# A Trainium2 encoder layer: the accumulating DMAs that make the weights' low parts read SBUF instead of DRAM, and make more of those parts

## The chip, the cores and the metric

The kernel runs on one core of one Trainium2 chip. The metric is the device time of one execution in microseconds (us), lower being better. The core has a matrix engine (PE, whose weight loads the profile lists apart as PEld), a vector engine (DVE), a scalar engine (ACT), a general engine (POOL) and a queue engine (SP) that here only issues DMAs. Every engine works through its own list of instructions in order, and semaphores tie the lists together. DMAs issued by SP, ACT and POOL share 16 DMA engines.

## What is computed

One layer of a bidirectional encoder is run on two requests with the same weights: the first request P has 512 tokens, the second, S, has 1024, with 1024 features each, all in float32.

```python
def encoder_layer(h, p_l, ...):
    u = group_rmsnorm(h, norm_mix_pre)
    proj = u @ w_in                              # 1024 x 5664: z, xBC, dt, hyena columns
    ...
    # SSD heads: depthwise conv + SiLU, chunked scans forward and backward,
    #   gate with silu(z), grouped norm
    # Hyena heads: depthwise conv, long convolution by FFT, grouped norm
    mix = jnp.concatenate([y_ssd, y_hy], axis=-1) @ w_out          # 2048 x 1024
    h = h + group_rmsnorm(mix, norm_mix_post)
    u = group_rmsnorm(h, norm_ffn_pre)
    ff = (jax.nn.silu(u @ w_gate) * (u @ w_up)) @ w_down           # hidden 2816
    h = h + group_rmsnorm(ff, norm_ffn_post)
    gate = jax.nn.sigmoid((group_rmsnorm(h, ple_norm_pre) @ w_ple_gate))
    e = p_l @ w_ple_proj
    return h + group_rmsnorm(gate * e, ple_norm_post)
```

## The kernel before

**Three products for one.** Every large matrix product is made of three. Each operand is split into a high part, its value rounded to the matrix format `F32R`, and a low part, what the rounding left. `mm3` (L296) then adds high times high, high times low and low times high in PSUM. On the activations' side `split_ps` (L324) makes the parts: the high one on ACT (L325), the low one on DVE (L326). On the weights' side there are two ways:

- `split_w` (L289): ACT copies the staging tile `wst` into `whi` (L292), and POOL subtracts, `wlo = wst - whi` (L293, a TENSOR_TENSOR).
- `split_dma` (L280): ACT writes `-wst`, rounded, into `wlo` (L284), then POOL issues a DMA with an adding destination that adds the exact weight on top (L285), and ACT copies `wst` into `whi` (L286). What is added comes from DRAM: the same rows of the weight that `wst` was loaded from.

`load_w` (L260) loads one block of a weight in two halves, each through `raw_w` (L275), a DMA of SP into a `wst` tile of 256 KB (128 partitions x 512 values). It chooses between the two ways: `split_w` where columns of another weight are put beside (`extra`, in `project_z` alone, 264 instead of 256 columns) or once `pool_lo` is set, else `split_dma`. `wst`, `whi` and `wlo` have six buffers each and are shared by the whole kernel, so a load must wait for whoever reads the tile six loads earlier.

**The stages.** First the projections of P, then of S, with `w_in` (192 tiles); beside them, as a second stream with PSUM of its own, the filters, the SSD scans and the long convolutions. From L1423 on the tail: P's output projection (`outproj`), P's FFN (`ffn`) beside the long convolution of S, then `pool_lo = True` (L1441), and the tail of S: the output projection in two groups of 512 tokens (`out_group`), P's embedding gate (`ple`) in between, gate and up products (`gate_up`, Strassen-like sums of weight blocks, which call `raw_w` and `split_w` themselves), the down projection (`down_group`), the embedding gates of S.

**The streamed products.** `out_group` and `down_group` go through `stream_gemm` (L1152). There the activations are loaded too: one row, a DMA of SP of 256 KB into one of two `mx` buffers (L1187), is split by ACT into `mh` and by DVE into `ml` (three buffers each), and takes part in 12 products with one weight tile. There are 152 rows: 64 in the output projection (2 groups x 2 halves of the columns x 16) and 88 in the down projection (2 x 2 x 22). SP issues the loads of `mx` and `wst` by turns.

The order of the instructions on each engine is made by the framework's scheduler when the program is built, from its own costs; tiles wait for each other by semaphores.

Of the kernel before, what the change touches and what calls it, by code (L numbers as in the profile page):

```python
# [15 lines left out]
ALU = mybir.AluOpType  # L16
# [66 lines left out]
class Whole:  # L83


    def __init__(self, his, los):
        self.parts, self.w = (his, los), his[0].shape[1]
# [79 lines left out]
class Kern:  # L167
    def __init__(self, ctx, tc, ins, outs, cst):
        self.ctx, self.tc, self.nc, self.I, self.cst = ctx, tc, tc.nc, ins, cst
        self.P = Seq("p", LP, ins["x_prompt"][0], ins["p_prompt"][0, 0], outs[0][0])  # L170
        self.S = Seq("s", LS, ins["x_sample"][0], ins["p_sample"][0, 0], outs[1][0])
        self.n = 0
        self.wide_tail = self.pool_lo = False
        for q in (self.P, self.S):
            d = lambda nm, shp: tc.dram_tile(shp, F32, name=f"{nm}_{q.nm}")
            L, R = q.L, q.R
            q.xs = d("xs", [L, 1024])
            q.z = d("z", [L, 1024])
            q.bt = d("bt", [2, 128, L])
            q.ct = d("ct", [2, 128, L])  # L180
            q.bk = d("bk", [L, 256])
            q.rows = d("rows", [2, q.nc, 16, 128])
            q.g = d("g", [R, 128, 1024])
            q.x0 = d("x0", [R, 128, 1024])
            q.K = d("K", [8, 128, R * 2 * 128])
            q.mix = d("mix", [16, 128, L])
            q.h1 = d("h1", [L, 1024])
            q.h2 = d("h2", [L, 1024])
            q.e = d("e", [L, 1024])
        self.S.hid = tc.dram_tile([NF, 128, LS], F32, name="hid_s")  # L190
# [69 lines left out]
    def load_w(self, src, a, b, extra=None):  # L260

        nc = self.nc
        rows = []
        n = max(1, a // 2)
        for k in range(0, a, n):
            ks = slice(k, k + n)
            w = src.shape[-1]
            st = self.raw_w(src[:, ks], b)
            if extra is not None:
                nc.gpsimd.tensor_copy(st[:, :, w:], extra[:, ks])  # L270
            hi, lo = self.split_w(st) if extra is not None or self.pool_lo else self.split_dma(st, src[:, ks])
            rows += [(hi[:, i], lo[:, i]) for i in range(n)]
        return rows

# [2 lines left out]
        self.nc.sync.dma_start(st[:, :, :src.shape[2]], src)  # L277
        return st

    def split_dma(self, w, src):  # L280

        nc = self.nc
        hi, lo = (self.T(self.wp, list(w.shape), t, F32R, 6) for t in ("whi", "wlo"))
        nc.scalar.activation(lo, w, AF.Copy, scale=-1.0)  # L284
        nc.gpsimd.dma_start(lo[:, :, :src.shape[2]], src, accum_op=ALU.add)  # L285
        nc.scalar.activation(hi, w, AF.Copy)  # L286
        return hi, lo

# [1090 lines left out]
    def build(self):  # L1379
# [40 lines left out]
        def tags(pool, *sizes):  # L1420
            return {t: (pool, t, n) for t, n in sizes}

        with self.pool("mix_s", side="right") as mp, ExitStack() as right:  # L1423
            pm = tags(mp, ("mx", 2), ("mh", 3), ("ml", 3))
            tr = right.enter_context(self.pool("out_s", side="right"))
            po = pm | tags(tr, ("acc", 4), ("row", 2), ("t4", 2), ("junk", 1), ("stage", 2), ("wsum", 1))
            with self.pool("tail_u") as tu, self.pool("tail_p") as tp:
                pl = tags(tu, ("et", 2), ("hh", 4), ("hl", 4), ("t4", 2), ("uh", 2), ("ul", 2))
                pl |= tags(tp, ("acc", 4), ("mst", 1), ("row", 2), ("junk", 1))
                pl["mx"] = pl["t4"]  # L1430
                pl["ga"] = pl["acc"]
                pt = self.ple_in(pl, [(S, 1)], True)
                mix = self.mix_in(P, 0, pl, 0, 8)
                self.ple_proj(pl, [(S, 1)], pt)
                acc = self.new_acc(pl)
                self.outproj(P, 0, pl, acc, 0, mix)
                pt = self.ple_in(pl, [(P, 0), (S, 0)])
                u = self.outproj(P, 0, pl, acc, 8, self.mix_in(P, 0, pl, 8, 8), lambda: self.new_u(pl, 4))
                self.ple_proj(pl, [(P, 0), (S, 0)], pt)
                u = self.ffn(P, 0, pl, u)  # L1440
                self.pool_lo = True  # L1441
                acc = self.new_acc(po)
                out = self.out_group(S, 0, po, acc)
                next(out)
                self.ple_post(P, 0, pl, self.ple(P, 0, pl, u))
            self.apool = self.pools["x"][0]
            next(out)
            with self.pool("blocks") as tb:
                pb = pm | tags(tb, ("bh", 14), ("bl", 14))
                po |= pb  # L1450
                us = [self.out_post(S, 0, po, acc)]
                acc = self.new_acc(po)
                for _ in self.out_group(S, 1, po, acc):
                    pass
                us.append(self.out_post(S, 1, po, acc))
                right.close()
                with self.pool("hid_s", side="right") as tr:
                    ph = pb | tags(tr, ("wsum", 3), ("sc", 5), ("gt", 6))
                    pe = pb | {"wsum": pm["mx"], "gt": pm["mh"], "sc": pm["ml"]}
                    both = dict(enumerate(us))  # L1460
                    self.gate_up(S, [(p, m, {g: both[g] for g in gs}) for p, gs, ms in (
                        (pe, [0], (0, 2)), (ph, [1], (0, 2)), (ph, [0, 1], range(4, NF, 2))) for m in ms])
                with self.pool("end_s", side="right") as tr:
                    pe = pb | tags(tr, ("row", 3), ("t4", 3), ("junk", 1), ("mst", 2))
                    pe |= {"acc": pe["bl"], "ga": pe["bh"]}
                    self.wide_tail = True
                    vs = [self.down_group(S, g, pe, lambda: Quarters(
                        *[[self.T(pe, [128, 4, 256], t, F32R) for _ in range(4)] for t in ("bh", "bl")]))
                        for g in range(2)]
                    for g in range(2):  # L1470
                        self.ple_post(S, g, pe, self.ple(S, g, pe, vs[g]))
# [30 lines left out]
```

## Time and profile before

| | |
|---|---|
| median of 3 runs | 2881.7 us (2876.18 to 2881.93) |
| the profiled execution | 2865.54 us, its span 2863.7 us, mean granted PE clock 0.977 |
| instructions in the span | 41893 |
| HBM read, written | 430.43 MB, 91.95 MB |

The profiled execution is 16.2 us (0.56%) faster than the median of the runs. Sums made from the profile are made against its 2865.54 us.

How to read it: the page gives the busy time of each engine, then the span in 40 slices of 71.6 us with the busy share in tenths. Roughly, slices 0 to 23 hold the projections and P's tail, 24 to 28 the output projection of S, 29 to 34 its gate and up products, 35 to 38 its down projection and embedding gates. Groups of instructions are named by line, engine, operation and by what they write and read. "mean ns" is the time of one. A wait row such as `PE g L301 <- ACT mh L325: 17.1, 8, 7.4` reads: PE sat idle before instructions of L301 until ACT's L325 had ended, 17.1 us in all, 8 times, 7.4 us at the longest. A name with a q behind it (SPq) is the engine's queue, which issues.

### The profile page before, as it was taken

Reading aid. Unit: us, or ns where it says so; the run is one execution under the profiler, and the core shown is the slowest. Engines: PE = TensorE matmul, PEld = TensorE weight load, DVE = VectorE, ACT = ScalarE, POOL = GpSimd, SP = SyncE. Lnnn points to the kernel's source line nnn. Section 1 sums busy time; section 2 is a strip of 40 time slices with the busy share of each in tenths; the row PEclk is TensorE's granted clock in tenths of the full one; section 3 lists DMA queues with packets and bytes.
Section 4 is the critical chain, followed back from the end, with each engine's and each line's share of the span. In section 5 each row is a group of like instructions: output and inputs, shape, how many; then the busy total and the mean of one; then the engine's idle time right before and its main releaser. Section 6 shows DMA issues by size and latency. Waiting matters only on the chain.

```text
span 2863.7 us, 41893 instructions
## 1 busy us (share of the span) xinstructions
PE 2682.8 (94%) x14696; PEld 2265.0 (79%) x14696; DVE 1696.4 (59%) x2905; ACT 1418.8 (50%) x2747; POOL 1388.6 (48%) x1147
## 2 busy tenths in 40 slices
PE   6999999999999988989999998989789999999998
PEld 5887898778888766777788776767689999877776
DVE  4675786886565684765576665365853434224345
ACT  5555545774335575674444454455543333345443
POOL 3444544343443443544465555554674445435464
PEclk8999999999999998989999999999899999999999
DMA  9799956978768898989999997475332222366665
GB/s 221 193 206 199 217 180 168 259 176 178 145 141 180 197 289 245 232 242 223 188 199 224 189 208 239 137 237 159 120 98 82 80 79 82 107 210 202 213 202 187
DMA packets 565261, 525.16 MB, mean 183 GB/s; under 512 B 31985, under 2 KB 455737, under 8 KB 562747
## 3 DMA queue, kind: packets, MB, share of 16 engines
q1 hardware_dynamic: 344523, 348.39, 40.2%
q0 software_dynamic: 141504, 112.22, 24.8%
q10 hardware_dynamic: 79024, 61.88, 6.7%
q8 instruction: 116, 1.90, 0.3%
q14 instruction: 94, 0.77, 0.1%
HBM read 430.43 MB, written 91.95 MB: 182 GB/s over the span
## 4 chain that ended last, share of the span: by engine, by line
PE 39%; DVE 7%; DMA 4%; issue 4%; POOL 2%; ACT 1%; SPq 0%; ACTq 0%; POOLq 0%; DVEq 0%
PE g L301 10%; PE g L303 10%; PE g L302 9%; PE a L301 2%; PE a L302 2%; PE a L303 2%; DMA mx<-mix_s 1%; PE a L700 1%; DVE ml L326 1%; PE a L973 1%; DVE b L692 1%; DMA b<-g_s 1%; POOL wlo L293 1%; DVE t L1055 1%; POOL rs_t L309 1%
## 5 line engine op out<-in xcount | busy, mean ns | idle before, releaser
L293 POOL TENSOR_TENSOR wlo<-wst,whi 128x512 fp32r<-128x512 f32 (+1 forms) x378 | 538.8, 1431 | 512.0 <-ACT whi L292 482.2
L301 PE MATMUL g<-uh,whi 128*128 128x512 f32 (+1 forms) x1232 | 494.5, 401 | 10.0 <-DVE cv L393 8.3
L302 PE MATMUL g<-ul,whi 128*128 128x512 f32 (+1 forms) x1232 | 491.9, 399 | 0.3 <-DVE ul L326 0.3
L303 PE MATMUL g<-uh,wlo 128*128 128x512 f32 (+1 forms) x1232 | 490.7, 399 | 0.0
L292 ACT ACTIVATE whi<-wst 128x512 fp32r<-128x512 f32 (+1 forms) x378 | 236.4, 629 | 356.6 <-PE g L302 193.2
L286 ACT ACTIVATE whi<-wst 128x512 fp32r<-128x512 f32 x316 | 197.5, 626 | 252.4 <-PE g L302 187.5
L301 PE MATMUL g<-bh,whi 128*128 128x256 f32 x1056 | 295.7, 285 | 22.7 <-DVE rs_t L308 6.8
L285 POOL DMA_DIRECT2D wlo<-in_w_in x144 | 188.7, 1377 | 245.8 <-ACT wlo L284 211.7
L303 PE MATMUL g<-bh,wlo 128*128 128x256 f32 x1056 | 295.4, 282 | 2.9 <-POOL wlo L293 2.9
L302 PE MATMUL g<-bl,whi 128*128 128x256 f32 x1056 | 296.5, 282 | 0.0
L301 PEld LDWEIGHTS g<-uh,whi 128*128 128x128 f32 x1232 | 233.9, 190 | 68.9 <-ACT cv L387 7.8
L302 PEld LDWEIGHTS g<-ul,whi 128*128 128x128 f32 x1232 | 233.4, 189 | 55.5 <-issue 7.0
L303 PEld LDWEIGHTS g<-uh,wlo 128*128 128x128 f32 x1232 | 232.9, 189 | 53.4 <-issue 5.1
L326 DVE TENSOR_TENSOR ml<-mx,mh 128x512 fp32r<-128x512 f32 x152 | 125.5, 827 | 222.2 <-ACT mh L325 222.2
L393 DVE SCALAR_TENSOR_TENSOR cv<-g,cols,cv 128x510 f32<-128x510 f32 (+3 forms) x192 | 193.9, 1010 | 100.6 <-ACT cv L387 98.3
L284 ACT ACTIVATE wlo<-wst 128x512 fp32r<-128x512 f32 x316 | 195.7, 620 | 94.2 <-PE g L302 86.0
L301 PEld LDWEIGHTS g<-bh,whi 128*128 128x128 f32 x1056 | 198.4, 190 | 29.2 <-DVE rs_t L308 7.1
L303 PEld LDWEIGHTS g<-bh,wlo 128*128 128x128 f32 x1056 | 200.6, 190 | 3.2 <-POOL wlo L293 3.2
L302 PEld LDWEIGHTS g<-bl,whi 128*128 128x128 f32 x1056 | 200.9, 190 | 0.1
L309 POOL TENSOR_TENSOR rs_t<-rs_t,nhalf 128x1 f32<-128x1 f32 (+2 forms) x112 | 127.2, 1137 | 149.1 <-DVE rs_t L308 148.5
L301 PE MATMUL g<-whi,uh 128*128 128x264 f32 (+1 forms) x576 | 192.8, 337 | 3.4 <-ACT acc L1097 3.4
L302 PE MATMUL g<-wlo,uh 128*128 128x264 f32 (+1 forms) x576 | 191.5, 333 | 3.1 <-DMA wlo<-in_w_out 3.1
(331 smaller groups left out, 6375.2 us busy)
## 6 DMA issues: line engine op xcount, KB each, us to landing
wst<-in_w_in SPq DMA_DIRECT2D x192, 256.0 KB
wlo<-in_w_in POOLq DMA_DIRECT2D x144, 256.0 KB, 6.0
wst<-in_w_down SPq DMA_DIRECT2D x132, 256.0 KB
wst<-in_w_out SPq DMA_DIRECT2D x96, 256.0 KB
wst<-in_w_gate SPq DMA_DIRECT2D x96, 256.0 KB
wst<-in_w_up SPq DMA_DIRECT2D x96, 256.0 KB
mx<-hid_s SPq DMA_DIRECT2D x88, 256.0 KB
rw<-rows_s SPq DMA_DIRECT2D x32, 512.0 KB
```

Source lines behind the costliest of these rows:

```text
L284: nc.scalar.activation(lo, w, AF.Copy, scale=-1.0)
L285: nc.gpsimd.dma_start(lo[:, :, :src.shape[2]], src, accum_op=ALU.add)
L286: nc.scalar.activation(hi, w, AF.Copy)
L292: nc.scalar.activation(hi, w, AF.Copy)
L293: (eng or nc.gpsimd).tensor_tensor(out=lo, in0=w, in1=hi.bitcast(F32), op=ALU.subtract)
L301: nc.tensor.matmul(ps, lh, rh, start=first, stop=False, skip_group_check=shared)
L302: nc.tensor.matmul(ps, lh, rl, start=False, stop=False, skip_group_check=shared)
L303: nc.tensor.matmul(ps, ll, rh, start=False, stop=last, skip_group_check=shared)
L309: nc.gpsimd.tensor_tensor(out=t[:, :w], in0=t[:, :w], in1=self.nhalf[:, :w], op=ALU.pow)
L326: self.nc.vector.tensor_tensor(out=lo, in0=ps, in1=hi.bitcast(F32), op=ALU.subtract)
L393: nc.vector.scalar_tensor_tensor(out[:, a:b], ps[:, a + d:b + d], wcol(w), out[:, a:b], ALU.mult, ALU.add)
L692: V.tensor_tensor(out=o, in0=a, in1=b, op=op)
```

## The change

`split_dma` no longer takes the DRAM source. The DMA adds the staging tile `wst` itself, from SBUF, onto `wlo`, whole rows at once. `load_w` always calls it, for `project_z` as well, where the tile has 264 columns, and in the tail of S; `pool_lo` is gone. `gate_up` is as it was.

```diff
-        self.wide_tail = self.pool_lo = False
+        self.wide_tail = False
...
-            hi, lo = self.split_w(st) if extra is not None or self.pool_lo else self.split_dma(st, src[:, ks])
+            hi, lo = self.split_dma(st)
             rows += [(hi[:, i], lo[:, i]) for i in range(n)]
...
-    def split_dma(self, w, src):
+    def split_dma(self, w):
         nc = self.nc
         hi, lo = (self.T(self.wp, list(w.shape), t, F32R, 6) for t in ("whi", "wlo"))
         nc.scalar.activation(lo, w, AF.Copy, scale=-1.0)
-        nc.gpsimd.dma_start(lo[:, :, :src.shape[2]], src, accum_op=ALU.add)
+        nc.gpsimd.dma_start(lo, w, accum_op=ALU.add)
         nc.scalar.activation(hi, w, AF.Copy)
         return hi, lo
...
                 u = self.ffn(P, 0, pl, u)
-                self.pool_lo = True
                 acc = self.new_acc(po)
```

In the built program POOL issues 316 adding DMAs before, 232 of them from DRAM rows of 512 bytes (128x4x128) and 84 from rows of 2 KB (128x512). In the changed one it issues 564: 516 of 128x512 and 48 of 128x528 (the z blocks). 248 subtractions on POOL go, 182 stay. ACT gets 248 more copies.

The first place is POOL's list in the first projections, where P's `project` runs; `w_in` is the weight in DRAM. Before:

```order
L285 DMA wlo_646<-in_w_in 128x4x128
L285 DMA wlo_653<-in_w_in 128x4x128
L285 DMA wlo_700<-in_w_in 128x4x128
L270 COPY wst_2682<-w_dt_121 128x2x8
L285 DMA wlo_707<-in_w_in 128x4x128
```

Now:

```order
L285 DMA wlo_646<-wst_643 128x512
L285 DMA wlo_653<-wst_650 128x512
L285 DMA wlo_700<-wst_697 128x512
L270 COPY wst_2682<-w_dt_121 128x2x8
L285 DMA wlo_707<-wst_704 128x512
```

The DMAs stand at the same places; four short rows a partition have become one long one, and the DMA reads the staging tile.

The second place is ACT's list in the first down projection of S (the first number in a name is the tile's, the same in both programs; `mx_4747` is a row of the activations, `wst_4768` the weight tile that is multiplied three rows later, with `mx_4762`). Before:

```order
L325 ACTIVATE mh_4748_25218<-mx_4747_25216 128x512
L292 ACTIVATE whi_4769_25284<-wst_4768_25282 128x512
L325 ACTIVATE mh_4751_25224<-mx_4750_25222 128x512
L292 ACTIVATE whi_4778_25326<-wst_4777_25324 128x512
L325 ACTIVATE mh_4760_25266<-mx_4759_25264 128x512
L292 ACTIVATE whi_4781_25332<-wst_4780_25330 128x512
```

Now:

```order
L325 ACTIVATE mh_4748_25380<-mx_4747_25378 128x512
L284 ACTIVATE wlo_4770_25450<-wst_4768_25447 128x512
L286 ACTIVATE whi_4769_25449<-wst_4768_25447 128x512
L325 ACTIVATE mh_4751_25386<-mx_4750_25384 128x512
L284 ACTIVATE wlo_4779_25493<-wst_4777_25490 128x512
L286 ACTIVATE whi_4778_25492<-wst_4777_25490 128x512
```

Behind each split of a row there stood one copy of a weight tile and now stand two.

The third place is SP's list in the same stretch (`wst_4804` is the load that takes the buffer of `wst_4768`, six loads earlier). Before:

```order
L277 DMA wst_4801_25420<-in_w_down 128x512
L1187 DMA mx_4759_25264<-hid_s_83 128x512
L277 DMA wst_4804_25426<-in_w_down 128x512
L1187 DMA mx_4762_25270<-hid_s_83 128x512
L277 DMA wst_4865_25618<-in_w_down 128x512
L1187 DMA mx_4771_25312<-hid_s_83 128x512
```

Now:

```order
L277 DMA wst_4801_25590<-in_w_down 128x512
L1187 DMA mx_4762_25434<-hid_s_83 128x512
L277 DMA wst_4804_25597<-in_w_down 128x512
L1187 DMA mx_4771_25478<-hid_s_83 128x512
L277 DMA wst_4865_25790<-in_w_down 128x512
L1187 DMA mx_4774_25484<-hid_s_83 128x512
```

The loads still alternate, but the row behind `wst_4804` is `mx_4771` instead of `mx_4762`: the weight loads have moved one row later. Rows of the activations follow each other in the order 4747, 4750, 4759, 4762, 4771, 4774.

## The prediction

> **What bounds the kernel now.** I read the page first, then busy time by stage, then PE's waits, then the timeline of one stage.
>
> ```profile
> PE 2682.8 (94%) x14696; PEld 2265.0 (79%) x14696; DVE 1696.4 (59%) x2905; ACT 1418.8 (50%) x2747; POOL 1388.6 (48%) x1147
> ...
> PE   6999999999999988989999998989789999999998
> ...
> DMA  9799956978768898989999997475332222366665
> ```
>
> PE is busy in 94% of the span, so all idle time of PE together is 2863.7 - 2682.8 = 181 us. What the change can win is a part of that, and what it can lose has no such bound. The DMA row is high up to slice 23 and falls to 2 to 7 tenths in the tail of S. The change takes DMA time out of the first region and puts new DMAs into the second. The stages in numbers (columns: us, busy time of PE, PEld, DVE, ACT, POOL with instructions, granted PE clock, DMA share, GB/s):
>
> ```profile
> 1432.00:1575.00 143.00, 142.91 (x715) 119.08 (x714) 102.62 (x168) 68.78 (x115) 83.31 (x56) 1.00 1.01 212
> ...
> 1718.00:2076.00 358.00, 307.10 (x1467) 250.21 (x1466) 210.22 (x242) 177.90 (x323) 196.69 (x158) 0.95 0.55 178
> ...
> 2506.00:2792.00 286.00, 271.51 (x1184) 217.71 (x1185) 115.62 (x138) 135.80 (x240) 145.21 (x115) 0.99 0.64 207
> ```
>
> P's FFN (first row) runs with its DMA engines at 1.01 and PE never idle, since its weights are loaded far ahead. The output projection of S with its surroundings (second row) leaves PE idle for 51 of 358 us at a DMA share of 0.55, the down projection and gates (third) for 15 of 286. Who ends PE's waits:
>
> ```profile
> PE g L301 <- ACT mh L325: 17.1, 8, 7.4
> PE g L303 <- DVE ml L326: 15.7, 6, 7.3
> ...
> PE g L302 <- DMA wlo<-in_w_down: 3.5, 4, 1.6
> ...
> PE g L302 <- DMA wlo<-in_w_out: 3.1, 3, 1.3
> ```
>
> The two longest, 32.8 us, are `mh` and `ml`, the streamed activations of S. The adding DMAs of the first half cost PE only 6.6 us. So the change acts on a small cost early and on the tightest loop late.
>
> **The early part: 316 adding DMAs read SBUF, z gets 48 more.** The 232 DMAs with 512-byte rows get rows of 2 KB.
>
> ```profile
> L285 POOL DMA_DIRECT2D wlo<-in_w_in x144 | 188.7, 1377 | 245.8 <-ACT wlo L284 211.7 <-ACT whi L286 9.5 <-DMA b<-g_p 6.2
> ...
> L285 POOL DMA_DIRECT2D wlo<-in_w_down x44 | 41.4, 999 | 67.2 <-ACT wlo L284 66.4 <-issue 0.8
> ...
> DMA to landing us min/median/max: 3.7/6.7/16.4
> ...
> q0 software_dynamic: 141504, 112.22, 24.8%
> ```
>
> POOL's issue of one falls from 1377 to about 999 ns: 232 x 0.38 = 88 us of POOL, which is under 50% busy, so nothing by itself. On the DMA engines, queue q0 holds them: 24.8% of 2863.7 us is 710 us for 112 MB, of which 83 MB are the 316 tiles; by bytes that is 1.66 us a tile on all 16 engines. If fewer packets save as much there as at the issue (999/1377), the 232 save some 0.45 us each, 105 us of 1700. That shortens waits for transfers; the two rows above sum to 6.6 us, and I take -6 us, between nothing and -15 (twice those waits, for the loads beside them).
>
> Against it stands a new wait. The staging buffer used to be free after two ACT copies; now it is held until the DMA has read it, 6.7 us later at the median, and the load that wants the buffer stands at the head of SP's list with everything behind it. P's FFN is where tiles follow fastest:
>
> ```profile
> 1602.36 0.62 ACT L284 ACTIVATE wlo<-wst 128x512 fp32r<-128x512 f32 x1
> ...
> 1603.00 0.34 SPq L277 DMA_DIRECT2D wst<-in_w_down  x1
> ...
> 1605.15 0.62 ACT L284 ACTIVATE wlo<-wst 128x512 fp32r<-128x512 f32 x1
> ```
>
> One tile every 2.79 us; a buffer comes round in six, 16.7 us. Landing (6.7) and a load of the same length (6.7 again) fill 13.4, so 3 us of cover are left for the weights. What is queued behind, the loads of the second stream, has no such cover. I take +6 us, from 0 to +20; the largest landing, 16.4 us, would eat the cover alone. The z blocks need no more than this: their tiles follow at half the pace. Early part: 0 in all, from -15 to +20.
>
> **The tail: 200 subtractions on POOL become adding DMAs.** A steady stretch of the down projection, PE's rows left out:
>
> ```profile
> 2580.03 0.63 ACT L325 ACTIVATE mh<-mx 128x512 fp32r<-128x512 f32 x1 [1.62 <-PE g L302]
> ...
> 2580.57 0.61 ACT L292 ACTIVATE whi<-wst 128x512 fp32r<-128x512 f32 x1
> ...
> 2580.70 0.69 DVE L326 TENSOR_TENSOR ml<-mx,mh 128x512 fp32r<-128x512 f32 x1 [2.08 <-ACT mh L325]
> ...
> 2581.26 1.29 POOL L293 TENSOR_TENSOR wlo<-wst,whi 128x512 fp32r<-128x512 f32 x1 [1.47 <-ACT whi L292]
> ...
> 2581.41 0.33 SPq L1187 DMA_DIRECT2D mx<-hid_s  x1
> ...
> 2582.58 0.33 SPq L277 DMA_DIRECT2D wst<-in_w_down  x1
> ...
> 2582.82 0.63 ACT L325 ACTIVATE mh<-mx 128x512 fp32r<-128x512 f32 x1 [1.64 <-PE g L302]
> ```
>
> One row and one weight tile every 2.79 us, paced by PE. SP issues a weight load as soon as POOL's subtraction ends (2581.26 + 1.29 = 2582.55), then the next `mx`. Before, a loop closes over three rows: `mh`, the copy 0.54 us later, the subtraction 0.69 after it for 1.29, SP's two issues, the load of `mx`, `mh` three rows on. It has 3 x 2.79 = 8.37 us and a load takes about 3 of them:
>
> ```profile
> 2566.45 0.33 SPq L1187 DMA_DIRECT2D mx<-hid_s  x1
> ...
> 2569.43 0.63 ACT L325 ACTIVATE mh<-mx 128x512 fp32r<-128x512 f32 x1 [1.55 <-DMA mx<-hid_s]
> ```
>
> Issue to use is 2.98 us, so there is room. After the change the link "POOL subtracts" is "an adding DMA lands". The lists show the loop over four rows: `mh_4748`, copy from `wst_4768`, its adding DMA, `wst_4804` in that buffer, `mx_4771`. Its fixed part is 0.54 to the copy, 0.69 to POOL, 0.35 of SP and little gaps, 1.65 us; on top come the landing and the load. Four rows have 11.16 us, so it holds PE up if **landing + load exceed 9.5 us**. At about a dozen places in the two streamed products the new lists close a loop over three rows, which have 8.37: there the limit is 6.7 us.
>
> Landing: at best 3.7 us (row above), 7.4 for 2 KB rows in P's FFN at a DMA share of 1.01, and between them at lighter load (the DMA issues of the window 1432 to 1575, then of 1370 to 1395, whose share follows):
>
> ```profile
> wlo<-in_w_down POOLq DMA_DIRECT2D x17, 256.0 KB, 7.4
> ...
> wlo<-in_w_down POOLq DMA_DIRECT2D x6, 256.0 KB, 5.1
> ...
> 1370.00:1395.00 25.00, 23.48 (x106) 18.90 (x104) 20.43 (x31) 9.45 (x17) 14.68 (x10) 1.00 0.83 166
> ```
>
> The tail has only 2 KB rows, two loads a row and no second stream, but its share would rise from 0.64 by 1.2 to 1.66 us in 2.79, to over 1. I take 5.5, nearer to the lighter row. Load: 2.98 undisturbed; in the output projection the chain that ended last already hangs on it at a share of 0.55:
>
> ```profile
> 1859.86 3.81 DMA mx<-mix_s
> ...
> 1865.13 5.09 DMA mx<-mix_s
> ...
> 1871.68 3.65 DMA mx<-mix_s
> ...
> 1876.80 2.97 DMA mx<-mix_s
> ```
>
> Their mean is 3.9; I take 3.7. The sum is 9.2: loops over four rows just close, each of the twelve over three rows loses 9.2 - 6.7 = 2.5 us: **+30 us**. At 3.7 + 2.98 nothing is lost; at 7.4 + 3.7 = 11.1 twelve lose 4.4 each and the remaining 29 loops of four rows 1.6 each, +99.
>
> What the tail wins: DVE's operations with two SBUF operands take longer while POOL subtracts.
>
> ```profile
> 2563.33 2.55 POOL L293 TENSOR_TENSOR wlo<-wst,whi 128x512 fp32r<-128x512 f32 x2 [0.72 <-ACT whi L292]
> ...
> 2564.91 1.51 DVE L326 TENSOR_TENSOR ml<-mx,mh 128x512 fp32r<-128x512 f32 x1 [1.75 <-ACT mh L325]
> ...
> L326 DVE TENSOR_TENSOR ml<-mx,mh 128x512 fp32r<-128x512 f32 x152 | 125.5, 827 | 222.2 <-ACT mh L325 222.2
> ...
> L1054 DVE SCALAR_TENSOR_TENSOR acc<-acc,rs_t,row 128x1024 f32<-128x1024 f32 x20 | 38.1, 1918 | 6.8 <-POOL rs_t L309 6.8
> ...
> L1054 DVE SCALAR_TENSOR_TENSOR acc<-acc,rs_t,row x20: 1270/1285/5880, 1197.6 to 2007.9; 128x1024 f32<-128x1024 f32 x20
> ```
>
> `ml` takes 1.51 us beside the subtraction and 0.69 alone; its mean is 827 ns, L1054's is 1918 against a least of 1270. Over all, 152 x 0.14 + 20 x 0.65 = 34 us of DVE. How much lies on the path, the chain of the window 1740 to 2080 tells, by line:
>
> ```profile
> by line: issue 11.4%; DMA mx<-mix_s 11.4%; PE g L303 10.0%; PE g L301 9.6%; PE g L302 9.1%; DVE ml L326 5.7%; PE a L302 3.5%; PE a L301 3.5%; DVE acc L1054 3.5%; PE a L303 3.4%; DVE bl L326 3.4%; DVE t L1055 3.1%; POOL wlo L293 2.2%; DVE ac
> ```
>
> `ml` and L1054 have 9.2% of 340 us, 31 us, of the 76 that they are busy there (64 rows at 0.83, some 12 times 1.92): 40%. So -14 us, from 0 to -34. ACT's 200 further copies of 0.62 us raise it from 135.8 to some 190 of 286 us; a row's split can queue behind one: +2 us, from 0 to +10.
>
> **Sum:** 0 + 30 - 14 + 2 = +18 us on the profiled 2865.5, that is 2883.5. The median of the runs stands 16.2 us above that execution, so I predict 2881.7 + 18 = 2900 us.
>
> **Rivals.** (1) The landing hides: if an addition out of SBUF lands in some 4 us, landing and load stay near 6.7 and no loop waits. Then the early relief without its wait (-6), half of DVE's 34 us (-17) and ACT's 2 are left, -21 us: 2861, faster. For it: the landings of 3.7 us, and no traffic of a second stream in the tail. Against it: the median of 6.7, and a DMA share that would pass 1. It decides below 7.5 us of landing and load, where twelve loops lose 10 us and the other terms win 12. The Trainium skill, "DMA: Bandwidth & Descriptors", section "Anatomy of one DMA — SWDGE (gpsimd) path", puts such a DMA at about 2.0 us plus its bytes at 436 GB/s; for 256 KB that is an estimate of 2.6 us, by which this rival would hold with room to spare, but no landing in this trace is under 3.7 us, so the trace speaks against the figure. (2) The tail's DMA engines saturate: landing 7.4 as in P's FFN, +99 - 14 + 2 = +87 us: 2969. For it the shares, against it that slower rows lower the load again. (3) The terms cancel: within 0.2%, 5.8 us, about what a measurement of this kernel can tell from no change: 2882. That the DMAs might keep their 512-byte rows is excluded by the lists (128x512).
>
> **How the numbers follow.** The forecast (the loops over three rows wait) gets 0.45, rival 2 0.15, rival 3 0.13, rival 1 0.27. Slower is 0.45 + 0.15 = 0.60, same 0.13, faster 0.27. The range from 2856 to 2946 holds the forecast, the cancelling, most of rival 1 and a third of rival 2. The forecast's own range is 2888 to 2932, +6 to +50.
>
> **What would show it.** Right: in the down projection SP's waits at L277 end with a landing of `wlo`, rows follow at more than 2.79 us in places, PE's waits for `mh` and `ml` grow from 32.8 to some 60 us, the median landing in the tail is 5 to 6 us, `ml` falls to about 0.69 us. Wrong: rows every 2.79 us throughout, landings under 4.5 us; or a DMA share near 1 and rows at 3.2 us and more (rival 2). In the early part the DMA share should fall by some 5 points while PE's idle time stays. The prediction also fails if loads of the second stream behind held buffers cost more than 20 us.

## The result, and the profile after

| | before | after |
|---|---|---|
| median of 4 runs each | 2881.81 us (2876.18 to 2886.2) | 2982.88 us (2970.14 to 2990.08) |
| ratio to before | | 1.0347, 95% interval 1.0306 to 1.0388: slower |
| profiled execution, its span | 2865.54, 2863.7 us | 2970.14, 2968.4 us |

The page of after, its rows of busy time, of PE and DMA by slice, and two lines that answer to those quoted of before:

```profile
PE 2719.9 (92%) x14696; PEld 2280.3 (77%) x14696; DVE 1613.0 (54%) x2905; ACT 1535.7 (52%) x2991; POOL 1152.9 (39%) x1147
...
PE   7999999999999989989999989887799999788987
...
DMA  9899978977567799978888899996332222899997
...
q0 software_dynamic: 88128, 177.64, 31.8%
...
L326 DVE TENSOR_TENSOR ml<-mx,mh 128x512 fp32r<-128x512 f32 x152 | 106.8, 706 | 331.3 <-ACT mh L325 329.5
```

PE's idle time grew from 181 to 248.5 us, and its busy time by another 37 us. In the two streamed products and the gates of S the DMA row now stands at 8 or 9 in most slices, where it stood at 4 to 7. `ml` became shorter, 706 ns in place of 827. Busy time by stage, the first block after, the second before (columns: us, busy time of PE, PEld, DVE, ACT, POOL with instructions, granted PE clock, DMA share, GB/s); rows: output projection of S, down projection, embedding gates, z of S:

```profile
1753.00:2044.00 291.00, 249.74 (x1029) 194.14 (x1028) 107.25 (x153) 166.87 (x303) 93.26 (x113) 0.95 0.93 247
...
2541.00:2850.00 309.00, 264.26 (x1069) 203.79 (x1070) 79.70 (x115) 162.87 (x298) 83.82 (x99) 0.93 0.95 244
2850.00:2968.00 118.00, 97.07 (x418) 76.90 (x416) 50.83 (x68) 62.79 (x115) 42.47 (x52) 0.93 0.88 255
362.00:515.00 153.00, 138.81 (x1003) 128.10 (x1002) 107.66 (x360) 78.27 (x186) 46.14 (x75) 0.97 0.80 212
```

```profile
1730.00:1996.00 266.00, 238.54 (x1026) 187.93 (x1025) 143.20 (x159) 129.69 (x230) 140.55 (x114) 0.98 0.60 194
...
2494.00:2758.00 264.00, 248.52 (x1069) 198.53 (x1070) 94.17 (x114) 119.40 (x210) 125.11 (x99) 0.99 0.64 202
2758.00:2864.00 106.00, 93.41 (x419) 75.62 (x417) 63.51 (x68) 48.95 (x87) 61.97 (x52) 0.96 0.57 204
352.00:488.00 136.00, 132.89 (x1004) 124.05 (x1002) 117.79 (x359) 67.52 (x162) 59.57 (x71) 1.00 0.56 174
```

Read the first number behind each window, then the last but one: four stages are longer by 25, 45, 12 and 17 us, and in each the DMA share rose to 0.80 to 0.95. z's first request lost another 10 us (112 to 174 before, 110 to 182 after). The gate and up products between the output and the down projection kept their 497 us; they use no adding DMA. PE's waits of after, columns as in the rows of waits quoted of before (`g` and `a` are two PSUM tiles that PE fills):

```profile
PE g L301 <- ACT mh L325: 48.9, 15, 13.1
PE a L301 <- ACT mh L325: 28.5, 18, 5.7
PE g L302 <- DMA wlo<-wst: 15.8, 10, 4.0
...
PE g L303 <- DVE ml L326: 3.2, 3, 1.7
```

Before there were, beside the two rows of `g` quoted in the prediction (17.1 and 15.7 us), two of `a`:

```profile
PE a L303 <- DVE ml L326: 2.8, 3, 1.0
...
PE a L301 <- ACT mh L325: 2.1, 3, 0.9
```

The waits for the streamed rows, `mh` and `ml` of both tiles, grew from 37.7 to 80.6 us; those for the landing of a low part itself stay small. What makes the rows late? The chain that ended last, in a stretch of the down projection of after (start, us, what):

```profile
2606.37 0.23 PE g L302
...
2615.22 6.61 DMA wlo<-wst
2621.89 0.33 SPq L277
2622.33 7.01 DMA mx<-hid_s
2629.43 0.64 ACT mh L325
2630.11 0.80 PE a L301
...
2631.76 0.43 PE a L302
```

Here it runs as the prediction said: a landing, the load of a weight tile that waited for it at the head of SP's list, and the load of `mx` behind it. But the load of `mx` is itself 7.01 us long. From SP's issue to the last packet these loads took 2.94 us at the median for `hid_s` before and 4.54 after, 3.43 and 4.61 for `mix_s` (worked out from the trace's DMA records). So there were two candidates: the buffer that is **held** until a landing, or the **traffic** that makes every load longer, whoever holds a buffer.

### The profile page after: what moved, and what is told of

The parts are those of the page before. It is cut to its first block, busy times and chain, and to the rows that moved or that the text cites. A ratio compares the mean times of both kernels' runs of the same rounds, so it can differ in the third digit from the quotient of the medians.

```text
span 2968.4 us, 42481 instructions
## 1 busy us (share of the span) xinstructions
PE 2719.9 (92%) x14696; PEld 2280.3 (77%) x14696; DVE 1613.0 (54%) x2905; ACT 1535.7 (52%) x2991; POOL 1152.9 (39%) x1147
## 4 chain that ended last, share of the span: by engine, by line
PE 53%; DMA 18%; issue 10%; DVE 10%; ACT 4%; POOL 3%; SPq 1%; ACTq 0%; POOLq 0%; DVEq 0%
PE g L301 15%; PE g L302 14%; PE g L303 14%; DMA wlo<-wst 6%; DMA mx<-mix_s 2%; DMA mx<-hid_s 2%; PE a L700 2%; PE a L973 1%; PE a L301 1%; POOL wlo L285 1%; PE a L302 1%; PE a L303 1%; DVE b L692 1%; PE a L404 1%; PE a L592 1%
## 5 line engine op out<-in xcount | busy, mean ns | idle before, releaser
L285 POOL DMA_DIRECT2D wlo<-wst x564 | 498.4, 924 | 998.5 <-ACT wlo L284 799.6
L286 ACT ACTIVATE whi<-wst 128x512 fp32r<-128x512 f32 (+1 forms) x564 | 352.2, 625 | 283.5 <-PE g L302 224.5
L284 ACT ACTIVATE wlo<-wst 128x512 fp32r<-128x512 f32 (+1 forms) x564 | 350.9, 622 | 177.6 <-PE g L302 134.9
L326 DVE TENSOR_TENSOR ml<-mx,mh 128x512 fp32r<-128x512 f32 x152 | 106.8, 706 | 331.3 <-ACT mh L325 329.5
L293 POOL TENSOR_TENSOR wlo<-wst,whi 128x512 fp32r<-128x512 f32 x130 | 185.4, 1429 | 195.4 <-ACT whi L292 150.7
L301 PE MATMUL g<-whi,mh 128*128 128x512 f32 x380 | 159.4, 419 | 50.7 <-ACT mh L325 48.9
L325 ACT ACTIVATE mh<-mx 128x512 fp32r<-128x512 f32 x152 | 94.8, 628 | 202.1 <-DMA mx<-hid_s 117.6
```

The lines of the kernel that those rows point to most:

```text
L285: nc.gpsimd.dma_start(lo, w, accum_op=ALU.add)
L293: (eng or nc.gpsimd).tensor_tensor(out=lo, in0=w, in1=hi.bitcast(F32), op=ALU.subtract)
L301: nc.tensor.matmul(ps, lh, rh, start=first, stop=False, skip_group_check=shared)
L325: self.nc.scalar.activation(hi, ps, AF.Copy)
L326: self.nc.vector.tensor_tensor(out=lo, in0=ps, in1=hi.bitcast(F32), op=ALU.subtract)
```

## The experiments

Each run's text of what was expected calls POOL GpSimd, ACT ScalarE and DVE VectorE. The stages in one table, in us, by first and last matmuls in the profile of each run. Gate, up and down are taken together, since in some kernels PE starts the down projection's first rows before the up product's end, in others behind it.

| kernel | z of S | output projection | gate, up, down | embedding gates | ratio to before, 95% interval |
|---|---|---|---|---|---|
| before | 136 | 266 | 761 | 106 | 1 |
| after | 153 | 290 | 806 | 119 | 1.0347 (1.0306 to 1.0388) |
| e1_early_only | 136 | 262 | 765 | 106 | 0.9992 (0.9975 to 1.0009) |
| e2_z_back | 136 | 295 | 817 | 117 | 1.0284 (1.0249 to 1.0318) |
| e3_tail_back | 157 | 266 | 762 | 107 | 1.0064 (1.0041 to 1.0086) |
| e4_tail_dram | 154 | 292 | 801 | 122 | 1.0320 (1.0273 to 1.0367) |
| e5_mx4 | 160 | 289 | 765 | 119 | 1.0198 (1.0179 to 1.0218) |
| e6_z_dve | 142 | 291 | 809 | 119 | 1.0330 (1.0301 to 1.0359) |
| e7_tail_act | 158 | 261 | 759 | 112 | 1.0056 (1.0038 to 1.0073) |
| e8_tail_ghost | 158 | 264 | 852 | 115 | 1.0383 (1.0355 to 1.0411) |
| e9_z_first | 141 | 295 | 816 | 120 | 1.0391 (1.0368 to 1.0415) |
| e10_z_second | 139 | 287 | 806 | 119 | 1.0276 (1.0253 to 1.0299) |
| e11_best_pool | 136 | 264 | 761 | 106 | 0.9977 (0.9962 to 0.9992) |
| e12_best_dma | 136 | 265 | 763 | 106 | 0.9987 (0.9975 to 1.0000) |
| e13_ghost4 | 159 | 262 | 831 | 108 | 1.0315 (1.0291 to 1.0338) |
| e14_mx3_out | 158 | 266 | 768 | 118 | 1.0134 (1.0108 to 1.0159) |
| e15_best_mx3 | 136 | 250 | 764 | 106 | 0.9937 (0.9916 to 0.9959) |
| e16_z_act | 142 | 290 | 804 | 120 | 1.0288 (1.0263 to 1.0313) |
| e17_best_shared | 136 | 252 | 754 | 106 | 0.9919 (0.9899 to 0.9939) |
| e18_mx3_shared | 155 | 268 | 770 | 120 | 1.0161 (1.0133 to 1.0190) |

### Which part costs what

e1_early_only keeps the subtraction for z and the tail; e2_z_back is after with z subtracted, e3_tail_back after with the tail subtracted.

```diff
-            hi, lo = self.split_dma(st)
+            hi, lo = self.split_w(st) if extra is not None or self.pool_lo else self.split_dma(st)   # e1
+            hi, lo = self.split_w(st) if extra is not None else self.split_dma(st)                   # e2
+            hi, lo = self.split_w(st) if self.pool_lo else self.split_dma(st)                        # e3
```

> Theory (the z blocks and the tail carry the whole loss; elsewhere reading the staging tile relieves the DMA engines): from the stage boundaries of the two traces, z of the first request lost about 10 us, z of the second 25 to 27, the stages from the second output projection to the end 81, together some 117 of which 101 came through, so the rest must have won 9 to 16 us. This kernel keeps only that part: 2866 to 2876 us, a ratio of 0.995 to 0.998. Rival (as the prediction had it, the relief is given back by loads that wait in SP's list for held buffers): 2882 us, a ratio of 1.000, and the stages up to the second output projection as long as before the change.

> This kernel is the changed one with z's low parts subtracted on GpSimd again, for both requests. Theory (z's adding DMAs cost 25 to 35 us, because a z tile's buffer comes back only after a landing that GpSimd's own next copy waits for): 2948 to 2960 us, a ratio of 1.023 to 1.027 to the kernel before, z of the second request in 136 us again instead of 153. Rival (z's loss at the boundaries is only a shift, taken back in the FFN behind it): 2975 to 2985 us, a ratio of 1.033 to 1.036.

> This kernel is the changed one with the tail (from the second request's output projection on) subtracted on GpSimd again. Theory (the tail costs 81 us): 2895 to 2910 us, a ratio of 1.005 to 1.010, with an output projection of 266, a down projection of 264 and gates of 106 us. Rival (the tail's loss comes in part from what the stages before it leave behind): above 2915 us.

The tail costs 1.0347 - 1.0064, 2.8% or 82 us. z costs 1.0064 - 0.9992, 0.7% or 21 us, taken the other way 1.0347 - 1.0284, 18 us. The early part gives 0.1% and its interval holds no change: the theory that the rest had won 9 to 16 us falls. P's FFN and what surrounds it, first before, then in e1:

```profile
1040.00:1730.00 690.00, 641.64 (x3088) 521.44 (x3087) 435.76 (x782) 365.15 (x728) 338.94 (x261) 0.96 0.95 222
```

```profile
1040.00:1730.00 690.00, 638.23 (x3063) 518.44 (x3062) 435.19 (x774) 363.03 (x720) 300.23 (x260) 0.96 0.87 224
```

The DMA share fell by 8 points (from 0.79 to 0.69 between 530 and 1030 us), POOL is busy 39 us less, and PE does nearly the same number of matmuls in the same time (3063 for 3088). What was relieved there was not what PE waited for.

### The tail: held buffer or traffic

e4_tail_dram takes the hold away and leaves the traffic; in the tail the adding DMA reads DRAM again:

```diff
-    def split_dma(self, w):
+    def split_dma(self, w, src):
...
-        nc.gpsimd.dma_start(lo, w, accum_op=ALU.add)
+        nc.gpsimd.dma_start(lo[:, :, :src.shape[2]], src, accum_op=ALU.add)
...
+            hi, lo = self.split_dma(st, src[:, ks] if self.pool_lo else st)
```

> The tail's adding DMAs read the weights in DRAM, so that a staging buffer comes free after ACT's two copies; number, size and bytes of the adding DMAs, ACT's copies and GpSimd's relief stay as in the changed kernel. Theory 1 (the buffer held until the landing closes the loop over SP's list): most of the 81 us of the tail come back, 2905 to 2935 us, a ratio of 1.008 to 1.018, and SP's waits for landings of wlo go away in the tail. Theory 2 (the added transfers slow the loads of mx and each other, whoever holds the buffer): 2970 to 2990 us, a ratio of 1.031 to 1.038, with mx loads at 4.5 us or more.

1.0320: about a tenth of the tail's loss came back, and the intervals of the two kernels overlap. So the loss doesn't need the held buffer. (The loads of `mx` took 4.6 us for `hid_s` and 5.0 for `mix_s` in e4, a little more than in after, so the hold may cost somewhat more than that tenth.) SP's waits in the tail, after first, then e4:

```profile
SPq L277 <- DMA wlo<-wst: 325.2, 153, 8.4
```

```profile
SPq L277 <- ACT whi L286: 178.3, 94, 8.9
SPq L1187 <- DVE ml L326: 144.0, 116, 4.0
```

The 325 us of SP waiting for landings are gone, and PE gained almost nothing. The chain of e4 shows what stands there in their place:

```profile
2632.47 0.53 ACT mh L325
2633.00 0.02 issue
2633.02 0.70 DVE ml L326
2633.74 5.51 DMA mx<-hid_s
2639.29 0.32 issue
2639.61 0.64 ACT mh L325
2640.25 0.02 issue
2640.28 0.70 DVE ml L326
2641.00 3.79 DMA mx<-hid_s
```

This is a loop over the two buffers of `mx`: load, `mh`, `ml`, and only then the load into the same buffer. One turn serves two rows, which take PE 5.58 us; from `ml` to `ml` it took 2640.28 - 2633.02 = 7.26 us. With a load of 2.98 and splits of 0.63 and 0.69 it takes some 4.4 us and hides. The trace of before shows this wait too, in SP's list over the tail:

```profile
SPq L1187 <- DVE ml L326: 153.6, 123, 6.5
```

Three experiments tell whether the loop carries the loss. e5_mx4 gives after four `mx` buffers from the down projection on, e7_tail_act has ACT's copies of after and an addition on POOL in place of the DMA, and e8_tail_ghost subtracts in the tail and, from the down projection on, starts a DMA per tile for nobody.

```diff
-                    pe = pb | tags(tr, ("row", 3), ("t4", 3), ("junk", 1), ("mst", 2))                  # e5
+                    pe = pb | tags(tr, ("row", 3), ("t4", 3), ("junk", 1), ("mst", 2), ("mx", 4))
...
+        nc.scalar.activation(lo, w, AF.Copy, scale=-1.0)                                                # e7
+        nc.gpsimd.tensor_tensor(out=lo, in0=w, in1=lo.bitcast(F32), op=ALU.add)
+        nc.scalar.activation(hi, w, AF.Copy)
...
+            if self.wide_tail:                                                                          # e8
+                self.turn += 1
+                nc.gpsimd.dma_start(self.spare[self.turn % 2][:, :n, :w], src[:, ks], accum_op=ALU.add)
```

> The changed kernel with four mx buffers in place of two from the down projection on (room is there only in that stage). Theory (traffic: an mx buffer's own loop of load, ACT split, DVE split has two rows, 5.58 us; the load grew from 2.9 to 4.5 us and with some 2 us of splits and queues passes that): the down projection falls from 308 to 265 to 285 us, the whole to a ratio of 1.019 to 1.027. Rival (staging buffers held until the adding DMA lands stop SP ahead of the loads of mx, so more mx buffers don't help): down stays at 300 to 310 us, ratio 1.032 to 1.037.

> In the tail ScalarE makes -w and w as in the changed kernel, and GpSimd adds w to -w in SBUF with a tensor operation where the change has the adding DMA: no added transfer. Theory 2 (traffic): against the changed kernel most of the 82 us of the tail come back, 2890 to 2915 us, a ratio of 1.004 to 1.013. Theory 3 (ScalarE's 200 further copies delay its splits of mx): the tail stays slow, above 2950 us, a ratio over 1.025.

> GpSimd subtracts in the whole tail, as before the change, and in the stage from the down projection on each weight tile also starts an adding DMA of 256 KB out of DRAM into a spare tile that nobody reads: traffic alone. Theory 2 (traffic): down rises from 264 to 290 to 315 us and the gates from 106 to 113 to 122, a ratio of 1.017 to 1.025 against the 1.006 of the kernel without these transfers. Rivals (the held buffer, or ScalarE's copies): down stays at 262 to 272 us, a ratio of 1.005 to 1.010.

e5 wins 41 us in gate, up and down; PE's waits and the busy times of its down projection:

```profile
PE g L301 <- ACT mh L325: 17.7, 1, 17.7
PE a L339 <- DVE bl L326: 3.9, 1, 3.9
...
2543.00:2819.00 276.00, 253.60 (x1091) 204.10 (x1091) 81.88 (x118) 165.03 (x301) 84.78 (x99) 0.96 1.03 282
```

One wait of 17.7 us for the first row is left (the four buffers come when the pool of the stage before closes) and none for `mh` after it. Yet the traffic is heavier than in after, a share of 1.03 against 0.95, and a load of `mx` took 5.9 us at the median. So PE loses next to nothing to long loads when enough rows are loaded ahead. By itself e5 doesn't tell the two loops apart: with four buffers the rows stand further ahead in SP's list, and in the built program the loop over a held staging buffer then closes mostly over six rows in place of four. That the held buffer isn't needed rests on e4 and on the transfers that hold nothing, in e8 and e13. In e7, with ACT's copies and no transfer, the two streamed products are as fast as before: ACT is not it. e8 is slow with transfers alone, but its down projection takes 356 us where 290 to 315 were expected, and POOL waited there for landings of the two spare tiles:

```profile
POOL spare L274 <- DMA spare<-in_w_down: 70.1, 41, 4.3
```

e13_ghost4 takes that out with four spare tiles (`self.turn % 4`). e14_mx3_out gives after three `mx` buffers in the output projection (and one gain row there, for room) beside e5's four:

```diff
-            pm = tags(mp, ("mx", 2), ("mh", 3), ("ml", 3))
+            pm = tags(mp, ("mx", 3), ("mh", 3), ("ml", 3))
...
-            po = pm | tags(tr, ("acc", 4), ("row", 2), ("t4", 2), ("junk", 1), ("stage", 2), ("wsum", 1))
+            po = pm | tags(tr, ("acc", 4), ("row", 1), ("t4", 2), ("junk", 1), ("stage", 2), ("wsum", 1))
```

> The tail subtracted on GpSimd, with the unread adding DMAs from the down projection on, as before, but into four spare tiles in place of two: with two, GpSimd itself waited 70 us in that stage for a spare tile's landing, which mixes a second cause in. If the traffic alone (through the loop of two mx buffers) slows the stage, down stays at 285 to 320 us and GpSimd's waits for landings fall below 15 us; if the blocked GpSimd made the 356 us, down falls to 262 to 275 us.

> The changed kernel with three mx buffers in the second request's output projection (room made by one gain row in place of two) and four from the down projection on. If the loop over mx's buffers carries the output projection's loss too: 264 to 276 us there in place of 290, the whole 1.009 to 1.016. If landings of wlo or held staging buffers carry it: 285 to 295 us, the whole 1.018 to 1.022. The single gain row may cost some us after each group.

In e13 POOL's wait for the spare tiles is down to 10.6 us:

```profile
POOL spare L274 <- DMA spare<-in_w_down: 10.6, 10, 2.1
...
PE g L304 <- ACT mh L328: 34.1, 19, 11.8
PE a L304 <- ACT mh L328: 18.0, 18, 2.5
```

The stage is still 70 us longer than without the transfers, and PE waits for `mh`, as in after. Traffic alone does it. Its down projection, 338 us, is even above what was expected and above after's 309; the loads of `mx` took 5.7 us at the median there against 4.5 in after, and why they did is open. e14's output projection is 266 us, what it was before the change, although loads of `mix_s` took 7.6 us at the median there. So the output projection's 24 us, too, are lost for want of rows loaded ahead; e14 opens both loops, as e5 does. e18_mx3_shared is after with the three buffers alone, shared by both products:

> The changed kernel with three shared mx buffers and nothing else altered. The two-buffer loop had 5.58 us, three have 8.37; a turn with the added transfers took some 6.5 to 7.3. If that loop is the cause: gate and up products with the down projection 755 to 770 us in place of 806, output projection 264 to 270 in place of 290, the whole 1.008 to 1.015. If four were needed because the loads themselves take 6 us and more at a full DMA share: 775 us and more, 1.016 to 1.022.

Output projection 268, gate, up and down 770: three buffers are enough for nearly all of it. The whole, 1.0161, is slightly above the range given and just inside the rival's, although the stages are not. Most of what is left over before is z and the gates.

### z

e6_z_dve moves the copy of the dt columns from POOL to DVE, e9_z_first and e10_z_second use the adding DMA for two of a column block's four tiles, and e16_z_act makes z's low parts by ACT's copy and POOL's addition, as e7 did in the tail.

```diff
-                nc.gpsimd.tensor_copy(st[:, :, w:], extra[:, ks])      # e6
+                nc.vector.tensor_copy(st[:, :, w:], extra[:, ks])
...
+            hi, lo = self.split_w(st) if sub else self.split_dma(st)    # e9: sub = kh == 1; e10: sub = kh == 0
...
+            hi, lo = self.split_add(st) if extra is not None else self.split_dma(st)    # e16
```

> The changed kernel with the copy of the eight dt columns into z's staging tile on VectorE in place of GpSimd. Theory (GpSimd's copy waits for the landing that frees the staging buffer and holds back the next adding DMAs behind it): z of the second request takes 136 to 142 us in place of 153, the whole a ratio of 1.028 to 1.032. Rival (the six buffers alone, held until landing, limit z): z 150 to 155 us, a ratio of 1.033 to 1.037.

> The changed kernel where of z's four staging tiles per column block the first two get their low part by the adding DMA and the last two (k-rows 4 to 7) by GpSimd's subtraction. Theory 5 (of six whi and wlo buffers two are ahead of PE; the third and fourth tile get theirs only in the last pass of the block before, so their low part stands on the path, and there the landing of 5 us takes the place of a subtraction of 1.4 to 2.5 us): with the late tiles on GpSimd z of the second request takes 136 to 142 us and the kernel 1.027 to 1.031. Rival (traffic or held staging buffers, in proportion to the number of adding DMAs): z about 145 us, 1.030 to 1.034.

> The other half: the first two tiles of a column block by GpSimd's subtraction, the last two by the adding DMA. Theory 5: z of the second request stays at 150 to 155 us, the ratio at 1.032 to 1.037. Rival (in proportion): z about 145 us, 1.030 to 1.034.

> The changed kernel where z's low part is made by ScalarE's copy of -w and GpSimd's addition in SBUF, without DMA. If the adding DMA (landing, traffic, held buffers) is what z loses by: z of the second request 134 to 140 us, a ratio of 1.025 to 1.030. If ScalarE's extra copies and their order are: 148 to 158 us, a ratio of 1.032 to 1.037.

The timeline of POOL in after, in a z block (the releaser of the idle time before each copy stands in brackets):

```profile
415.19 0.20 POOL L270 COPY wst<-w_dt 128x16 f32<-128x16 f32 x1 [2.30 <-DMA wlo<-wst]
417.88 0.20 POOL L270 COPY wst<-w_dt 128x16 f32<-128x16 f32 x1 [2.49 <-DMA wlo<-wst]
422.25 0.20 POOL L270 COPY wst<-w_dt 128x16 f32<-128x16 f32 x1 [4.17 <-DMA wlo<-wst]
```

POOL's copy into a staging buffer waits for that buffer's landing, and the next adding DMAs stand behind it. With the copy on DVE z of S takes 142 us, as that theory said, though the whole missed its range. Without the DMA (e16) z takes 142 as well, between the two ranges given and near the first, and the whole is back at e2's ratio. So 11 of the 17 us that z of S lost go with the DMA, and with POOL's copy that waits for it; the other 6 are there without any DMA, beside ACT's added copies, and were not taken apart further. But either half also brings z to 139 to 141 us, so the theory of the late tiles falls (its rival, in proportion, had said 145), and the whole does not follow the stage: e9, with z at 141, is the slowest of all, and e6 and e9 gave their gain back before the output projection (1264 and 1259 us from z's end to there, against 1238 after). The scheduler orders the work between the two in another way in each of these kernels: of PE's 8440 matmuls ahead of the output projection, 428 to 740 stand elsewhere in the traces than in after's. **What makes z slow is shown for the larger part, what of it reaches the end is not**: 18 to 21 us with all four tiles on the DMA, anything from none to more than all of it with part of them.

### A faster kernel

If a loop over two buffers of `mx` is that close to its limit, it may bind before the change too. e11_best_pool is e1 with e5's four buffers, e12_best_dma the same with adding DMAs in the down projection, e15_best_mx3 is e11 with e14's three buffers, and e17_best_shared is e15 without the four new ones.

> The kernel before with the early source change alone and four mx buffers from the down projection on, the tail and z subtracted on GpSimd. By the traffic theory the mx loop over two rows seldom binds here (load 2.9 us): down 258 to 264 us in place of 264, the whole 0.994 to 1.000. If more buffers are worth something even without added transfers (chain of before hangs on mx there): down below 256 us.

> As the kernel with four mx buffers and the early source change, but the down projection's low parts by adding DMAs. Four mx buffers with adding DMAs gave 258 us for down in an earlier run here. If the relief of VectorE and GpSimd is worth something once the mx loop is open, down is 252 to 260 us and the whole 0.992 to 0.998, below the kernel with the subtraction; if it is not, both agree within 0.2%.

> The kernel with the early source change alone and four mx buffers from the down projection on, with three mx buffers in the output projection as well (one gain row). Where the loop over two mx buffers holds up the output projection before the change too (the chain that ended last hangs on mx there), 262 falls to 250 to 258 us and the whole to 0.993 to 0.997; if not, or if the single gain row gives it back, 0.997 to 1.001.

> The kernel with the early source change alone and three mx buffers that the output projection and the down projection share, in place of three and then four new ones. New buffers come only when the pool of the stage before closes: PE waits 18.4 us in one piece for the first row of the down projection there. If the shared buffers let that row load ahead, gate and up products with the down projection fall from 764 to 745 to 755 us and the whole to 0.986 to 0.992. If three buffers are too few there, or the wait has another cause: 0.992 to 0.997.

e11 and e12 agree: with the loop open, the adding DMA is worth nothing against the subtraction in that stage, on balance and with DVE's relief included. Three buffers take 12 to 16 us out of the output projection. The wait of 18.4 us for the first row, e15's largest, is gone in e17, whose waits for the rows are

```profile
PE g L303 <- DVE ml L326: 11.8, 10, 2.2
...
PE g L301 <- ACT mh L325: 3.2, 1, 3.2
```

e17 beats both kernels, the one before by 0.8%: 2853.5 us, a ratio of 0.9919 (0.9899 to 0.9939).

## Why the prediction was wrong

The direction was right, the size was not: 18 us forecast, 101 measured, beyond the range.

- **Early part, 0 us: right, z left out.** e1 measures 0.9992, no change. Its two terms, -6 us of relief and +6 us of new waits, were not measured apart.
- **"The z blocks need no more than this: their tiles follow at half the pace": wrong.** z costs 18 to 21 us. Before the change z of S used 32 tiles in 136 us, one every 4.25 us, where half the pace of P's FFN would be 5.6. The step also priced SP's list alone and not POOL's, where the copy of the dt columns waits for the same landing ahead of the next adding DMAs; taking that copy off POOL gave back 11 of z's 17 us (e6).
- **"loops over four rows just close, each of the twelve over three rows loses 9.2 - 6.7 = 2.5 us": the step that failed.** It put the tail's cost, +30 us, on one loop, over the held staging buffer, with a load of 3.7 us; the two streamed products lost 69. The load was mis-sized: 4.5 to 4.6 us were measured with the hold, and 5.6 to 7.6 where more buffers let PE keep its pace, although the step itself says that the DMA share would pass 1. With the measured landing and load, 10.2 together, its own sum would have been 12 x 3.5 + 29 x 0.7 = 62 us. In the built program more places close over three rows than the dozen taken, too: 26 of the 88 weight tiles of the down projection and 33 of the 64 of the output projection. And the loop was not the one that the loss needs. Its signs came true: SP waited 325 us for landings in the tail, the median landing was 5.5 us in the down and 5.8 in the output projection, as taken, and PE's waits for the rows grew beyond the 60 us named. But e4 removed this loop and recovered about a tenth. A sign that fits a theory doesn't tell that its wait decides. The longer load stands in a second loop, over the two `mx` buffers, which the prediction did not write down though its wait stood in SP's rows. In after both loops are near their limit; what the held buffer would cost without the longer loads, no run shows.
- **Rival 2, 2969 us, had the cause but not the way:** the engines did fill up, to 0.93 to 0.95, but landings stayed at 5.5 to 5.8 and not 7.4, and the loss ran through the loads of `mx`.
- **DVE's relief, -14 us: nothing seen.** `ml` did fall to 706 ns, and e12 is no faster than e11. Its share of a chain was taken as time on the path; the loop's load grew by 1.2 to 1.6 us where `ml` shrank by 0.12.
- **ACT's copies, +2 us: small, as said, for the two products** (e7, at 261 and 759 us, is no slower than e3). In the gates e7 shows some 5 us more than e3.
- **The gates, not priced: 13 us.** With ACT's copies alone they take 112 us, with traffic alone 108 (e13) to 115 (e8), with the adding DMA 117 to 122 whatever `mx` has. What makes up the rest was not tried.

Added up: some 24 us in the output projection, 45 in the down projection, 13 in the gates, about 20 in z; the middle gave nothing.

## What to carry to other kernels

Before adding traffic, list every loop that a load stands in, one per buffer tag, with its turn and the rows that it covers, and put the longer load into each; a queue's wait for an engine that reads the buffer is the row that shows such a loop. Removing a suspected wait and seeing no gain is worth more than seeing the wait in the trace. One more buffer on a loop near its limit can be worth more than an engine's relief: here it took back more than half of the loss (e18, 1.0161 in place of 1.0347), and without the change it made the kernel faster.

## What the hardware showed beyond that

A stall of PE costs more than its length. Stretches of 11 us of after's down projection (columns as above; the clock stands before the DMA share):

```profile
2541.00:2552.00 11.00, 10.07 (x42) 7.81 (x42) 2.41 (x4) 6.90 (x14) 4.33 (x5) 1.00 0.85 199
2552.00:2563.00 11.00, 0.00 (x0) 0.00 (x0) 0.00 (x0) 0.41 (x1) 0.87 (x1) 0.66 1.06 315
2563.00:2574.00 11.00, 9.41 (x31) 7.54 (x32) 2.68 (x4) 4.61 (x8) 1.57 (x2) 0.71 0.78 243
2574.00:2585.00 11.00, 11.00 (x49) 8.85 (x48) 2.77 (x4) 6.05 (x11) 2.53 (x4) 1.00 0.99 245
```

PE stands idle in the second stretch; in the third it is busy for 9.41 us but does 31 matmuls where the fourth does 49, at a granted clock of 0.71. In the chain quoted of after, matmuls follow each other at 0.23 us ahead of the stall and at 0.43 behind it. The down projection's busy time grew by 16 us (248.5 to 264.3) for the same 1069 matmuls, beside 29 us of added idle time; its mean granted clock fell from 0.99 to 0.93, and 248.5 x 0.99 / 0.93 = 264.5.

Kernels with the same work in the tail differ there, too. From the output projection to the end after takes 1215 us, and e10, where PE's 6256 matmuls stand in the same order, 1212; e2 and e9, where 32 and 25 of them stand elsewhere, take 1229 and 1231. Whether the order makes these 15 us or the meeting of the transfers, at a DMA share over 0.9, is not shown; differences of that size between two such kernels' tails were not read as effects.
